# Differential attention: a running maximum over the chunks of keys, and two maps combined without dividing by the first sum

## The chip, the core and the metric

The kernel runs on one core of one Trainium2 chip. The metric is the device time of one execution in microseconds (us). Three runs of the kernel before gave 3016.61, 3018.57 and 3020.60 us, median 3018.57. The engines are named as the profile names them: PE (matmul) with PEld (its weight loads), DVE (vector), ACT (scalar, activations), POOL (general purpose, vector-like), and SP, whose queue issues all DMAs.

## What is computed

One decoder layer: a shared norm, one input projection, two token mixers side by side (sliding-window attention and differential attention), an output projection, cross-attention into a memory of 256 tokens, and a squared-ReLU MLP. Only the differential attention changes. It has 4 heads, 2048 tokens, two score maps per head and values of width 128:

```python
s = jnp.einsum('bqhcd,bkhcd->bhcqk', qblk, k) * scale      # c = 0, 1: two maps
s = jnp.where(mask, s, -jnp.inf)                           # causal
p = jax.nn.softmax(s, axis=-1)
a = p[:, :, 0] - lam * p[:, :, 1]
od = jnp.einsum('bhqk,bkhe->bqhe', a, v)
out_b = rms_norm(od, g_diff) * (1.0 - lam_init)            # per head, eps 1e-5
```

## The kernel before

The program runs in phases: the input projection, attention, the output projection (`phase_out`), cross-attention, the MLP up and down. Attention is cut into 32 units, one for a head `h` and a block `s` of 256 query tokens (`units`; heads 0 and 2 go through the blocks upwards, 1 and 3 downwards). A unit has one to four chunks `j` of at most 512 keys (`nch` chunks; two blocks of each head have one chunk, two have two, two three, two four) and two halves `t` of 128 queries.

**Scores** (`softmax`, L485 to L497). For every (j, t) and both maps c, PE makes scores into a PSUM bank `sc` (two matmuls, in the last chunk a third, L490, for the mask). DVE takes the row maximum, negated, into `nm` (L491), ACT makes exp(score - maximum) into `p[:, c]` and its row sum `l` (L492). There are four banks with the tag `s`; the score tiles of the window attention (`wsc`, L614) use them too. So the fifth score tile can only be begun when the exponential of the first has been read out of its bank.

**Weighing** (`weigh`). When all chunks of a unit are through, small DVE instructions on a few columns take the maximum over the chunks (L509), ACT makes the correction factors (L511), DVE the total sum and its reciprocal (L512 to L514), minus lambda into the second map's factor (L517), and the factors `scl` (L519). Then POOL multiplies the second map of every (j, t) by its factor (L524), and DVE adds the first map times its factor (L531). For the pairs in the table `POOL` both steps are done on POOL (L526, L527).

**Values** (`values`). PE transposes the combined map (L556), ACT and DVE copy it, in split form for some blocks (`af`; `ah` and `al`, L563, L142, L143), and PE multiplies by the values (L546). A sum of squares per token goes through POOL (L575) and PE (`pss`, L579) into `ss_d`. `phase_out` reads it back for every 512 tokens (`dss`), makes 1/sqrt(mean + eps) (`rsqrt_mean`, L157 to L163), stores it (`rs_d`), reads it back as rows (`rb`) and multiplies the attention output by it before the output projection (`po`, L807).

These steps, those of 32 window units (`window_softmax`, with the small L627 and L632, and `window_values`) and of 16 memory columns are laid out by due times in `phase_attention` (`at(...)`); a scheduler then sets the order in which the instructions stand on each engine. Each engine runs its own in that order.

Of the kernel before, what the change touches and what calls it, by code (L numbers as in the profile page):

```python
# [18 lines left out]
P = 128  # L19
# [47 lines left out]
class K:  # L67
# [77 lines left out]
            nc.scalar.activation(hi, src, AF.Copy, scale=scale)  # L145
            nc.vector.scalar_tensor_tensor(lo, src, scale, f(hi), op0=ALU.mult, op1=ALU.subtract)  # L146

    def rsqrt_mean(self, ss, n, out):

        nc = self.nc  # L150
        p, w = ss.shape
        if w == 512:
            v, y, t = (self.win(name=x) for x in ("rs_v", "rs_y", "rs_t"))
        else:
            v, y, t = (self.tiny_pool.tile([p, w], F32, name=x, tag=f"{x}{w}", bufs=1) for x in ("rs_v", "rs_y", "rs_t"))
        i = t.bitcast(I32)
        nc.vector.tensor_scalar(v, ss, 1.0 / n, EPS, op0=ALU.mult, op1=ALU.add)  # L157
        nc.vector.tensor_scalar(i, v.bitcast(I32), 1, None, op0=ALU.logical_shift_right)
        nc.vector.tensor_scalar(y.bitcast(I32), i, -1.0, float(0x5F3759DF), op0=ALU.mult, op1=ALU.add)
        for it in range(3):  # L160
# [277 lines left out]
def phase_attention(k, mt):  # L438
# [18 lines left out]
    def softmax(i, h, s, res):  # L457
# [17 lines left out]
        for j, w in enumerate(chunks):  # L475
            kt = kv[h, j][0]
            for t in range(2):
                last = j == nch - 1
                u = w - P if last and t == 0 else w
                um = max(u, 256)  # L480
                p = k.main([P, 2, 512], F32, name="p")
                for c in range(2):
                    sc = k.ps("s", name="sc")
                    for x in range(2):
                        mm = nc.tensor.matmul(  # L485
                            sc[:, :um], q[:, x, c, P * t : P * t + P], kt[:, c, :um], start=(x == 0), stop=(x == 1 and not last)
                        )
                        started.setdefault(i, mm)
                    if last:
                        nc.tensor.matmul(sc[:, u - P : u], k.identb, k.tri, start=False, stop=True)  # L490
                    nc.vector.tensor_reduce(nm[:, t, j, c : c + 1], sc[:, :u], axis=AX.X, op=ALU.max, negate=True)  # L491
                    nc.scalar.activation(  # L492
                        p[:, c, :u], sc[:, :u], AF.Exp, bias=nm[:, t, j, c : c + 1], accum_out=l[:, t, j, c : c + 1]
                    )
# [6 lines left out]
    def weigh(h, s, chunks, pt, nm, l):  # L501

        nch = len(chunks)
        sc = k.small([P, 2, 4, 2], "scl")[:, :, :nch]
        r = k.small([P, 2, 1, 2], "r")
        swap = "p t j c -> p t c j"
        if nch > 1:
            bm = k.small([P, 2, 1, 2], "bm")
            nc.vector.tensor_reduce(bm.rearrange(swap), nm.rearrange(swap), axis=AX.X, op=ALU.min)  # L509
            nc.vector.tensor_tensor(sc, bm.broadcast_to([P, 2, nch, 2]), nm, op=ALU.subtract)  # L510
            nc.scalar.activation(sc, sc, AF.Exp)  # L511
            nc.vector.tensor_tensor(l, l, sc, op=ALU.mult)  # L512
            nc.vector.tensor_reduce(r.rearrange(swap), l.rearrange(swap), axis=AX.X, op=ALU.add)
            nc.vector.reciprocal(r, r)  # L514
        else:
            nc.vector.reciprocal(r, l)
        nc.vector.tensor_scalar(r[:, :, :, 1], r[:, :, :, 1], k.nlam, None, op0=ALU.mult)  # L517
        if nch > 1:
            nc.vector.tensor_tensor(sc, sc, r.broadcast_to([P, 2, nch, 2]), op=ALU.mult)  # L519
        else:  # L520
            sc = r
        each = [(j, t, *pt[t, j]) for j in range(nch) for t in range(2)]
        for j, t, p, u in each:
            nc.gpsimd.tensor_tensor(p[:, 1, :u], p[:, 1, :u], sc[:, t, j, 1:2].broadcast_to([P, u]), op=ALU.mult)  # L524
            if (j, t) in POOL:
                nc.gpsimd.tensor_tensor(p[:, 0, :u], p[:, 0, :u], sc[:, t, j, 0:1].broadcast_to([P, u]), op=ALU.mult)  # L526
                nc.gpsimd.tensor_tensor(p[:, 0, :u], p[:, 0, :u], p[:, 1, :u], op=ALU.add)  # L527
        yield
        for j, t, p, u in each:
            if (j, t) not in POOL:  # L530
                nc.vector.scalar_tensor_tensor(  # L531
                    p[:, 0, :u], p[:, 0, :u], sc[:, t, j, 0:1], p[:, 1, :u], op0=ALU.mult, op1=ALU.add
                )
            yield
# [236 lines left out]
def phase_out(k, after):  # L771
# [6 lines left out]
    gd = k.small([P, 1], "gd", bufs=1)  # L778
    nc.vector.tensor_scalar(gd, k.g_diff, 1.0 - LAM_INIT, None, op0=ALU.mult)
    for c in CHUNKS:  # L780
        ss, rs = k.small([64, 32], "dss", bufs=2), k.small([64, 32], "drs", bufs=2)
        k.load(ss, k.ss_d[c].rearrange("h (a b) -> (h a) b", b=32))
        k.rsqrt_mean(ss, 128, rs)
        nc.sync.dma_start(k.rs_d[c].rearrange("o h (a b) -> (o h a) b", b=32), rs)
        o = [k.main([P, 2, 512], F32, name="o") for _ in range(4)]
        rb = [k.main([P, 2, 512], F32, name="rb") for _ in range(2)]
# [449 lines left out]
def build(nc, tc, a, out):  # L1236
# [3 lines left out]
    with ExitStack() as es:  # L1240
# [4 lines left out]
        k.vs_d = dram("vs_d", P, NT, P)  # L1245
        k.cs_d = dram("cs_d", 2, 32, S)
        k.ow_d, k.od_d = ([dram(f"{n}{i}", 4, P, 512) for i in range(4)] for n in ("ow_d", "od_d"))
        k.ss_d = [dram(f"ss_d{i}", 4, 512) for i in range(4)]
        k.rs_d = [dram(f"rs_d{i}", 1, 4, 512) for i in range(4)]
        k.kv_d = [[dram(f"kv_d{x}{i}", P, 4, MEM) for i in range(4)] for x in range(2)]  # L1250
        k.mt_d = [[dram(f"mt_d{x}{i}", P, 4, MEM) for i in range(2)] for x in range(2)]
# [100 lines left out]
```

## Time and profile before

| what | us |
|---|---|
| median of three runs | 3018.57 |
| the profiled execution | 3016.24 |
| its span, first to last instruction | 3014.5 |
| attention with its tail, 424 to 1036 us from the start | 612 |
| PE, DVE, ACT, POOL busy in these 612 us | 544.1, 491.1, 409.3, 378.2 |

A span row tells how long an engine was busy in a stretch; a wait row tells for whom an engine stood still; the chain of waits goes back from the last instruction to what released each step. The profiled execution lies 2.3 us below the median of the runs.

### The profile page before, as it was taken

The numbers are of one execution on the slowest core, as the hardware profiler recorded it, in microseconds if no ns is written. First come the engines' busy times: TensorE is split into PE (matmuls) and PEld (weight loads), VectorE is DVE, ScalarE is ACT, GpSimd is POOL, SyncE is SP. The second block draws the span as 40 slices with busy tenths as digits, with TensorE's granted clock in tenths as the row PEclk, the third lists the DMA queues.
The fourth block names the chain that finished last, engine by engine and source line by source line (L and its number), as shares of the span: only waits on it lengthen the run. The fifth ranks groups of instructions, "written<-read, shape, count | busy, mean of one in ns | idle before, by whom it ended". The sixth has DMA issues, their size and how long they took to land.

```text
span 3014.5 us, 38737 instructions
## 1 busy us (share of the span) xinstructions
PE 2882.1 (96%) x13740; PEld 2349.5 (78%) x13740; DVE 1762.1 (58%) x2918; ACT 1124.7 (37%) x2481; POOL 1161.8 (39%) x914
## 2 busy tenths in 40 slices
PE   8999988989999899999998999999999999999996
PEld 8978866666666688888886788778888888888886
DVE  5254448887788642422357765755556666666656
ACT  7221137666776521434324343533342111111113
POOL 0133336665666543112225666575551100110015
PEclk9999989999999999999998999999999999999997
DMA  8443264425342464211347553533345222212203
GB/s 313 133 179 127 108 195 123 126 72 154 114 122 85 156 203 166 93 49 44 117 134 247 181 178 112 177 124 112 110 151 214 73 68 77 77 60 74 77 7 112
DMA packets 223296, 380.21 MB, mean 126 GB/s; under 512 B 25312, under 2 KB 95104, under 8 KB 223104
## 3 DMA queue, kind: packets, MB, share of 16 engines
q1 hardware_dynamic: 223104, 377.75, 37.6%
q8 instruction: 108, 1.77, 0.2%
q14 instruction: 84, 0.69, 0.1%
HBM read 259.65 MB, written 116.98 MB: 125 GB/s over the span
## 4 chain that ended last, share of the span: by engine, by line
PE 61%; DVE 6%; DMA 3%; POOL 2%; issue 2%; ACT 1%; SPq 0%; POOLq 0%; DVEq 0%; ACTq 0%
PE pd L1194 23%; PE p L1102 18%; PE sc L871 6%; PE po L807 5%; PE po L995 4%; DMA xs<-x_d 1%; PE sc L485 1%; DVE p L531 1%; PE o L546 1%; PE wo L662 1%; PE pv L937 1%; PE pq L831 1%; DVE nm L491 1%; POOL p L524 1%; PE tt L556 1%
## 5 line engine op out<-in xcount | busy, mean ns | idle before, releaser
L1102 PE MATMUL p<-xh,w 128*128 128x512 f32 x1792 | 560.6, 394 | 22.4 <-DVE w L1093 11.2
L1198 DVE TENSOR_TENSOR acc<-pd,acc 128x512 f32<-128x512 f32 (+1 forms) x520 | 350.9, 681 | 254.0 <-PE pd L1194 251.4
L1102 PEld LDWEIGHTS p<-xh,w 128*128 128x128 f32 x1792 | 339.1, 190 | 99.3 <-DVE w L1093 13.7
L1194 PE MATMUL pd<-uh,wdh 128*128 128x512 f32 (+1 forms) x1040 | 401.7, 386 | 1.0 <-DVE acc L1198 1.0
L1194 PE MATMUL pd<-ul,wdh 128*128 128x512 f32 (+1 forms) x1040 | 401.2, 386 | 0.0
L1194 PE MATMUL pd<-uh,wdl 128*128 128x512 f32 (+1 forms) x1040 | 401.2, 386 | 0.0
L1102 PE MATMUL p<-xl,w 128*128 128x512 f32 x896 | 351.6, 392 | 0.0
L118 POOL TENSOR_TENSOR wdl<-wf,wdh 128x1024 fp32r<-128x1024 f32 x32 | 77.6, 2424 | 549.5 <-ACT wdh L117 543.6
L492 ACT ACTIVATE p<-sc,nm 128x512 f32<-128x512 f32 (+3 forms) x320 | 198.7, 627 | 94.1 <-DVE nm L491 92.8
L485 PE MATMUL sc<-kt,q 128*128 128x512 f32 (+2 forms) x640 | 198.6, 413 | 33.7 <-ACT p L492 23.1
L1194 PEld LDWEIGHTS pd<-uh,wdh 128*128 128x128 f32 x1040 | 195.4, 188 | 40.3 <-DVE acc L1198 1.2
L1194 PEld LDWEIGHTS pd<-ul,wdh 128*128 128x128 f32 x1040 | 195.4, 188 | 39.2
L1194 PEld LDWEIGHTS pd<-uh,wdl 128*128 128x128 f32 x1040 | 195.4, 188 | 39.2
L491 DVE TENSOR_REDUCE nm<-sc 128x1 f32<-128x512 f32 (+3 forms) x320 | 184.0, 600 | 53.4 <-PE sc L490 30.3
L1102 PEld LDWEIGHTS p<-xl,w 128*128 128x128 f32 x896 | 170.2, 190 | 35.8 <-issue 0.2
L485 PEld LDWEIGHTS sc<-kt,q 128*128 128x128 f32 x640 | 108.3, 198 | 85.5 <-ACT p L492 45.1
L524 POOL TENSOR_TENSOR p<-p,scl 128x512 f32<-128x512 f32 (+3 forms) x144 | 151.3, 1079 | 52.8 <-DVE scl L519 40.7
L142 ACT CAST uh<-uf 128x1024 fp32r<-128x1024 f32 x64 | 65.8, 1049 | 276.4 <-PE pd L1194 263.7
L306 PE MATMUL pa<-hh,wh 128*128 128x512 f32 x416 | 162.2, 390 | 0.2 <-DVE mt L146 0.2
L306 PE MATMUL pa<-hl,wh 128*128 128x512 f32 x416 | 162.1, 390 | 0.0
L306 PE MATMUL pa<-hh,wl 128*128 128x512 f32 x416 | 161.7, 389 | 0.0
L173 POOL TENSOR_TENSOR tot<-tot,sq 128x512 f32<-128x512 f32 x56 | 78.8, 1408 | 188.0 <-ACT sq L172 186.5
(266 smaller groups left out, 6046.0 us busy)
## 6 DMA issues: line engine op xcount, KB each, us to landing
wf<-w_up SPq DMA_DIRECT2D x64, 512.0 KB
u_d<-u SPq DMA_DIRECT2D x128, 256.0 KB
uf<-u_d SPq DMA_DIRECT2D x64, 512.0 KB
qk_d<-rot SPq DMA_DIRECT2D x96, 256.0 KB
x_d<-x SPq DMA_DIRECT2D x32, 512.0 KB
x<-x_d SPq DMA_DIRECT2D x32, 512.0 KB
xs<-x_d SPq DMA_DIRECT2D x32, 512.0 KB
wf<-w_down SPq DMA_DIRECT2D x32, 512.0 KB
```

Of the source, the lines that this page charges most:

```text
L173: getattr(nc, eng).tensor_tensor(total, total, sq, op=ALU.add)
L306: nc.tensor.matmul(pa, s_[d // 4][:, P * (d % 4) : P * (d % 4) + P], hs(m_, c, d), start=(d == 0 and i == 0), stop=(d == DT - 1 and i == 2),)
L485: mm = nc.tensor.matmul(sc[:, :um], q[:, x, c, P * t : P * t + P], kt[:, c, :um], start=(x == 0), stop=(x == 1 and not last))
L491: nc.vector.tensor_reduce(nm[:, t, j, c : c + 1], sc[:, :u], axis=AX.X, op=ALU.max, negate=True)
L492: nc.scalar.activation(p[:, c, :u], sc[:, :u], AF.Exp, bias=nm[:, t, j, c : c + 1], accum_out=l[:, t, j, c : c + 1])
L524: nc.gpsimd.tensor_tensor(p[:, 1, :u], p[:, 1, :u], sc[:, t, j, 1:2].broadcast_to([P, u]), op=ALU.mult)
L807: nc.tensor.matmul(po, wo[d][s_][:, P * n : P * n + P], m_[d // 2][:, d % 2], start=(d == 0 and z == 0), stop=(d == 7 and z == 2))
L871: nc.tensor.matmul(sc[n], x[s_][d][:, ts], wq[d][m_][:, 512 * n : 512 * n + 512], start=(d == 0 and z == 0), stop=(d == DT - 1 and z == 2))
L995: nc.tensor.matmul(po[i], vw[b][s_][:, P * n : P * n + P], m_[b], start=(b == 0 and z == 0), stop=(b == 7 and z == 2))
L1102: mm = nc.tensor.matmul(ps, t[:, s_, P * d : P * d + P], x[d][m_], start=(d == 0 and z == 0), stop=(d == 3 and z == 2))
L1194: nc.tensor.matmul(pd, w[ft][s_][:, P * n : P * n + P], u[m_][:, ft, ts], start=(ft == 0 and z == 0), stop=(ft == 1 and z == 2))
L1198: nc.vector.tensor_tensor(av, pd, av, op=ALU.add)
```

## The change

Maxima run on: from the second chunk on, DVE takes the smaller of this chunk's negated maxima and those of the chunk before (`nm`, both maps in one 128x2 instruction, 96 of them). So both maps' scores of a (j, t) are made first, then both maxima, then that minimum, then both exponentials. The last chunk's maximum is that of the whole row, so its correction factor is 1.

The maps are combined without dividing by the first sum: the result is l0 times the difference, with second factor -lambda * l0 / l1. The norm behind it takes up the factor if its eps is multiplied by l0 squared; l0 (`sums`) is stored to `l_d` by a DMA of 256 single numbers for each unit (32 of them), read back in `phase_out` (`dl`, 4 loads), squared and multiplied by eps. The last chunk is combined by one DVE instruction for each half; POOL's multiplications (L524) are 96 where they were 160. The table `POOL` names (2, 1) where it named (3, 1), and is asked only for chunks before the last, so 8 pairs of 256 columns go from POOL to one DVE instruction each (136 such instructions where there were 128).

```diff
-        nc.vector.tensor_scalar(v, ss, 1.0 / n, EPS, op0=ALU.mult, op1=ALU.add)
+        if eps is None:
+            nc.vector.tensor_scalar(v, ss, 1.0 / n, EPS, op0=ALU.mult, op1=ALU.add)
+        else:
+            nc.vector.scalar_tensor_tensor(v, ss, 1.0 / n, eps, op0=ALU.mult, op1=ALU.add)
...
+                both = []
                 for c in range(2):
                     sc = k.ps("s", name="sc")
+                    both.append(sc)
...
                     nc.vector.tensor_reduce(nm[:, t, j, c : c + 1], sc[:, :u], axis=AX.X, op=ALU.max, negate=True)
+                if j:
+                    nc.vector.tensor_tensor(nm[:, t, j], nm[:, t, j], nm[:, t, j - 1], op=ALU.min)
+                for c, sc in enumerate(both):
                     nc.scalar.activation(
...
-            nc.vector.tensor_reduce(bm.rearrange(swap), nm.rearrange(swap), axis=AX.X, op=ALU.min)
-            nc.vector.tensor_tensor(sc, bm.broadcast_to([P, 2, nch, 2]), nm, op=ALU.subtract)
+            nc.vector.tensor_tensor(sc, nm[:, :, nch - 1 :].broadcast_to([P, 2, nch - 1, 2]), nm[:, :, old], op=ALU.subtract)
...
-        nc.vector.tensor_scalar(r[:, :, :, 1], r[:, :, :, 1], k.nlam, None, op0=ALU.mult)
+        nc.vector.reciprocal(r[:, :, 1], sums[:, :, 1])
+        nc.vector.scalar_tensor_tensor(r[:, :, 1], r[:, :, 1], k.nlam, sums[:, :, 0], op0=ALU.mult, op1=ALU.mult)
...
+        nc.sync.dma_start(k.l_d[s // 2][h, cs].rearrange("(t p) -> p t", p=P), sums[:, :, 0])
         each = [(j, t, *pt[t, j]) for j in range(nch) for t in range(2)]
         for j, t, p, u in each:
-            nc.gpsimd.tensor_tensor(p[:, 1, :u], p[:, 1, :u], sc[:, t, j, 1:2].broadcast_to([P, u]), op=ALU.mult)
+            if j < nch - 1:
+                nc.gpsimd.tensor_tensor(p[:, 1, :u], p[:, 1, :u], sc[:, t, j, 1:2].broadcast_to([P, u]), op=ALU.mult)
...
         for j, t, p, u in each:
-            if (j, t) not in POOL:
+            if j == nch - 1:
+                nc.vector.scalar_tensor_tensor(p[:, 0, :u], p[:, 1, :u], r[:, t, 1:2], p[:, 0, :u], op0=ALU.mult, op1=ALU.add)
+            elif (j, t) not in POOL:
...
+        k.load(l, k.l_d[c].rearrange("h (a b) -> (h a) b", b=32))
+        nc.vector.scalar_tensor_tensor(l, l, EPS, l, op0=ALU.mult, op1=ALU.mult)
+        k.rsqrt_mean(ss, 128, rs, l)
```

What this does to the order shows at three places. Lines after the first edit are shifted in the changed kernel: L491 becomes L496, L492 becomes L500, L509 to L519 become L517 to L525, L531 becomes L538 (last chunk) and L540 (others), L118 and L143 stay.

On DVE at the end of the scores of head 0, block 6 (four chunks; `nm_4530`, in the changed kernel `nm_4532`, holds its maxima, `wl` belongs to a window unit), before:

```order
L491 TENSOR_REDUCE nm_4530<-sc_4736 128x1
L634 TENSOR_TENSOR wl_4636<-wl_4636,we_4637 128x4
L491 TENSOR_REDUCE nm_4530<-sc_4742 128x1
L635 RECIPROCAL wl_4636<-wl_4636 128x4
L491 TENSOR_REDUCE nm_4530<-sc_4750 128x1
L491 TENSOR_REDUCE nm_4530<-sc_4756 128x1
L509 TENSOR_REDUCE bm_4788<-nm_4530 128x4
```

and now:

```order
L498 TENSOR_TENSOR nm_4532<-nm_4532 128x2
L496 TENSOR_REDUCE nm_4532<-sc_4742 128x1
L496 TENSOR_REDUCE nm_4532<-sc_4747 128x1
L498 TENSOR_TENSOR nm_4532<-nm_4532 128x2
L496 TENSOR_REDUCE nm_4532<-sc_4757 128x1
L496 TENSOR_REDUCE nm_4532<-sc_4762 128x1
L498 TENSOR_TENSOR nm_4532<-nm_4532 128x2
L517 TENSOR_TENSOR scl_4795<-nm_4532 128x2x6
```

Two maxima are now followed by a minimum that reads both, and the reduction L509 is gone.

On ACT, in the first two chunks of the same unit (`sc` are score banks; `af` and `ah` are copies for the values of the unit before), before:

```order
L492 ACTIVATE p_4532,l_4531<-sc_4533,nm_4530 128x512
L563 COPY af_4488<-tt_4483 128x512
L492 ACTIVATE p_4532,l_4531<-sc_4538,nm_4530 128x512
L492 ACTIVATE p_4554,l_4531<-sc_4555,nm_4530 128x512
L142 CAST ah_4548<-tt_4543 128x512
L492 ACTIVATE p_4554,l_4531<-sc_4560,nm_4530 128x512
```

and now:

```order
L500 ACTIVATE p_4534,l_4533<-sc_4535,nm_4532 128x512
L500 ACTIVATE p_4534,l_4533<-sc_4539,nm_4532 128x512
L500 ACTIVATE p_4556,l_4533<-sc_4557,nm_4532 128x512
L500 ACTIVATE p_4556,l_4533<-sc_4561,nm_4532 128x512
L590 COPY row_4673<-pss_4671 1x256
L572 COPY af_4705<-tt_4700 128x512
L500 ACTIVATE p_4626,l_4533<-sc_4627,nm_4532 128x512
L500 ACTIVATE p_4626,l_4533<-sc_4631,nm_4532 128x512
```

Before, other work stood between the two exponentials of a pair; now they stand together.

On DVE at the end of attention, where the norm of the differential output begins (`dss` is the loaded sum of squares, `drs` the result, `al` the last split copy for the values, `wol` and `ol` belong to the output projection), before:

```order
L118 TENSOR_TENSOR wol<-wf,woh 128x1024
L163 SCALAR_TENSOR_TENSOR drs<-rs_t,rs_y 64x32
L157 TENSOR_SCALAR rs_v<-dss 64x32
L158 TENSOR_SCALAR rs_t<-rs_v 64x32
L159 TENSOR_SCALAR rs_y<-rs_t 64x32
L161 TENSOR_TENSOR rs_t<-rs_y 64x32
L162 SCALAR_TENSOR_TENSOR rs_t<-rs_t,rs_v 64x32
L163 SCALAR_TENSOR_TENSOR rs_y<-rs_t,rs_y 64x32
L161 TENSOR_TENSOR rs_t<-rs_y 64x32
L162 SCALAR_TENSOR_TENSOR rs_t<-rs_t,rs_v 64x32
L143 TENSOR_TENSOR al<-tt,ah 128x512
```

and now:

```order
L118 TENSOR_TENSOR wol<-wf,woh 128x1024
L166 SCALAR_TENSOR_TENSOR drs<-rs_t,rs_y 64x32
L143 TENSOR_TENSOR al<-tt,ah 128x512
L793 SCALAR_TENSOR_TENSOR dl<-dl 64x32
L143 TENSOR_TENSOR ol<-o,oh 128x1024
L160 SCALAR_TENSOR_TENSOR rs_v<-dss,dl 64x32
```

The last `al` stood behind the second `dss`; now it stands ahead of the second `dl`.

## Rows read from the trace of the kernel before

**Rows 1.** The page: the profiled execution's span.
```profile
span 3014.5 us, 38737 instructions
```

**Rows 2.** Busy time by stretch; columns are in the first line.
```profile
core 0: us, PE busy (x) PEld busy (x) DVE busy (x) ACT busy (x) POOL busy (x), PEclk, DMA share, GB/s
424.00:1036.00 612.00, 544.11 (x2974) 393.69 (x2973) 491.05 (x1025) 409.26 (x1260) 378.16 (x383) 0.95 0.41 120
...
719.00:1032.00 313.00, 282.20 (x1573) 204.03 (x1574) 252.18 (x531) 213.77 (x651) 195.25 (x201) 0.98 0.42 123
...
628.00:662.00 34.00, 27.15 (x134) 19.80 (x132) 30.53 (x52) 19.08 (x59) 25.59 (x27) 0.88 0.12 31
```

**Rows 3.** Waits, 424 to 1036 us: us in total, times, longest.
```profile
ACT p L492 <- DVE nm L491: 92.8, 90, 3.8
...
PEld sc L485 <- ACT p L492: 45.1, 51, 2.7
...
PE sc L485 <- ACT p L492: 23.1, 28, 2.5
...
DVE p L531 <- POOL p L524: 6.9, 10, 1.3
```

**Rows 4.** Groups by line, 424 to 1036: busy us, mean ns | idle before.
```profile
L491 DVE TENSOR_REDUCE nm<-sc 128x1 f32<-128x512 f32 x224 | 146.2, 679 | 27.9 <-PE sc L485 21.8 <-PE sc L490 5.7
L531 DVE SCALAR_TENSOR_TENSOR p<-p,scl 128x512 f32<-128x512 f32 x84 | 100.5, 1210 | 3.4 <-POOL p L524 3.3
...
L627 DVE TENSOR_TENSOR wnm<-wnm,nsink 128x2 f32<-128x2 f32 x64 | 21.7, 340 | 0.4
...
L524 POOL TENSOR_TENSOR p<-p,scl 128x512 f32<-128x512 f32 x108 | 123.0, 1163 | 52.8 <-DVE scl L519 40.7 <-DMA wk<-qk_d 7.4 <-DVE we L632 4.6
...
L526 POOL TENSOR_TENSOR p<-p,scl 128x256 f32<-128x256 f32 x8 | 7.1, 889 | 0.0
L527 POOL TENSOR_TENSOR p<-p 128x256 f32<-128x256 f32 x8 | 6.3, 784 | 0.0
```

**Rows 5.** Line 627, all instructions: duration ns min/median/max, first and last start.
```profile
L627 DVE TENSOR_TENSOR wnm<-wnm,nsink x64: 141/160/1839, 428.5 to 1000.7; 128x2 f32<-128x2 f32 x64
```

**Rows 6.** Timeline around 820 us: start, us, instruction [idle before].
```profile
815.55 3.72 DVE L531 SCALAR_TENSOR_TENSOR p<-p,scl 128x512 f32<-128x512 f32 x3
...
820.13 0.73 DVE L531 SCALAR_TENSOR_TENSOR p<-p,scl 128x512 f32<-128x512 f32 x1
820.79 1.27 DVE L491 TENSOR_REDUCE nm<-sc 128x1 f32<-128x512 f32 x2
...
821.50 0.69 ACT L492 ACTIVATE p<-sc,nm 128x512 f32<-128x512 f32 x1 [3.69 <-DVE nm L491]
...
822.33 0.73 PE L485 MATMUL sc<-kt,q 128*128 128x512 f32 x2 [0.78 <-ACT p L492]
```

**Rows 7.** The chain of waits, 719 to 1032 us, by line (shares of the stretch).
```profile
by line: PE sc L485 10.9%; DVE p L531 10.7%; PE o L546 8.5%; PE wo L662 6.9%; DVE nm L491 5.9%; issue 5.6%; POOL p L524 5.3%; PE tt L556 5.3%; ACT p L492 3.6%; PE pk L762 2.8%; DVE al L143 2.6%; DMA wq<-qk_d 2.2%; PE wsc L614 2.1%; DMA q<-q
```

**Rows 8.** Busy time by stretch of single lines: L531 (DVE), then L524 (POOL).
```profile
719.00:1032.00 313.00, 72.93 (x66) 0.98 0.42 123
...
424.00:1036.00 612.00, 163.37 (x160) 0.95 0.41 120
```

**Rows 9.** Timeline of the end of attention, by engine.
```profile
1025.05 0.38 PE L546 MATMUL o<-ah,v 128*128 128x256 f32 x1 [0.68 <-ACT ah L142]
1030.70 0.58 PE L546 MATMUL o<-al,v 128*128 128x256 f32 x1 [5.27 <-DVE al L143]
...
1087.55 1.05 PE L182 MATMUL col<-ones,tot 128*128 128x1 f32 x8 [0.60 <-POOL tot L173]
...
1028.37 0.17 DVE L157 TENSOR_SCALAR rs_v<-dss 64x32 f32<-64x32 f32 x1 [2.68 <-DMA dss<-ss_d]
...
1029.52 1.04 ACT L142 CAST oh<-o 128x1024 fp32r<-128x1024 f32 x1 [4.53 <-DMA o<-ow_d]
...
1025.13 0.27 SPq L582 DMA_DIRECT2D ss_d<-row  x1
```

More of the change, by code (lines that the diff above doesn't have):

```diff
@@ L42 @@
 CHUNKS = (3, 2, 1, 0)
-POOL = ((1, 1), (3, 1))
+POOL = ((1, 1), (2, 1))
 WHOLE = (0, 2, 4, 6)
@@ L146, in split, with rsqrt_mean @@
             nc.vector.scalar_tensor_tensor(lo, src, scale, f(hi), op0=ALU.mult, op1=ALU.subtract)
-    def rsqrt_mean(self, ss, n, out):
+    def rsqrt_mean(self, ss, n, out, eps=None):
         nc = self.nc
@@ L503, in weigh @@
         nch = len(chunks)
-        sc = k.small([P, 2, 4, 2], "scl")[:, :, :nch]
-        r = k.small([P, 2, 1, 2], "r")
-        swap = "p t j c -> p t c j"
+        r, sums = k.small([P, 2, 2], "r"), l[:, :, 0]
+        sc = None
         if nch > 1:
-            bm = k.small([P, 2, 1, 2], "bm")
-            nc.vector.tensor_reduce(bm.rearrange(swap), nm.rearrange(swap), axis=AX.X, op=ALU.min)
-            nc.vector.tensor_tensor(sc, bm.broadcast_to([P, 2, nch, 2]), nm, op=ALU.subtract)
+            old = slice(0, nch - 1)
+            sc = k.small([P, 2, 4, 2], "scl")[:, :, old]
+            nc.vector.tensor_tensor(sc, nm[:, :, nch - 1 :].broadcast_to([P, 2, nch - 1, 2]), nm[:, :, old], op=ALU.subtract)
@@ L511, in weigh @@
             nc.scalar.activation(sc, sc, AF.Exp)
[L512 to L516, printed above, removed]
-        nc.vector.tensor_scalar(r[:, :, :, 1], r[:, :, :, 1], k.nlam, None, op0=ALU.mult)
+            nc.vector.tensor_tensor(l[:, :, old], l[:, :, old], sc, op=ALU.mult)
+            sums = k.small([P, 2, 2], "ls")
@@ L518, in weigh @@
+            nc.vector.tensor_reduce(sums, l.rearrange("p t j c -> p t c j"), axis=AX.X, op=ALU.add)
+        nc.vector.reciprocal(r[:, :, 1], sums[:, :, 1])
+        nc.vector.scalar_tensor_tensor(r[:, :, 1], r[:, :, 1], k.nlam, sums[:, :, 0], op0=ALU.mult, op1=ALU.mult)
         if nch > 1:
-            nc.vector.tensor_tensor(sc, sc, r.broadcast_to([P, 2, nch, 2]), op=ALU.mult)
-        else:
-            sc = r
+            nc.vector.tensor_tensor(sc[:, :, :, 1], sc[:, :, :, 1], r[:, :, 1:].broadcast_to([P, 2, nch - 1]), op=ALU.mult)
@@ L522, in weigh @@
+        cs = slice(256 * (s % 2), 256 * (s % 2) + 256)
+        nc.sync.dma_start(k.l_d[s // 2][h, cs].rearrange("(t p) -> p t", p=P), sums[:, :, 0])
         each = [(j, t, *pt[t, j]) for j in range(nch) for t in range(2)]
         for j, t, p, u in each:
-            nc.gpsimd.tensor_tensor(p[:, 1, :u], p[:, 1, :u], sc[:, t, j, 1:2].broadcast_to([P, u]), op=ALU.mult)
-            if (j, t) in POOL:
-                nc.gpsimd.tensor_tensor(p[:, 0, :u], p[:, 0, :u], sc[:, t, j, 0:1].broadcast_to([P, u]), op=ALU.mult)
-                nc.gpsimd.tensor_tensor(p[:, 0, :u], p[:, 0, :u], p[:, 1, :u], op=ALU.add)
+            if j < nch - 1:
+                nc.gpsimd.tensor_tensor(p[:, 1, :u], p[:, 1, :u], sc[:, t, j, 1:2].broadcast_to([P, u]), op=ALU.mult)
+                if (j, t) in POOL:
+                    nc.gpsimd.tensor_tensor(p[:, 0, :u], p[:, 0, :u], sc[:, t, j, 0:1].broadcast_to([P, u]), op=ALU.mult)
+                    nc.gpsimd.tensor_tensor(p[:, 0, :u], p[:, 0, :u], p[:, 1, :u], op=ALU.add)
@@ L780, in phase_out @@
     for c in CHUNKS:
-        ss, rs = k.small([64, 32], "dss", bufs=2), k.small([64, 32], "drs", bufs=2)
+        ss, l, rs = (k.small([64, 32], n, bufs=b) for n, b in (("dss", 1), ("dl", 1), ("drs", 2)))
         k.load(ss, k.ss_d[c].rearrange("h (a b) -> (h a) b", b=32))
-        k.rsqrt_mean(ss, 128, rs)
+        k.load(l, k.l_d[c].rearrange("h (a b) -> (h a) b", b=32))
+        nc.vector.scalar_tensor_tensor(l, l, EPS, l, op0=ALU.mult, op1=ALU.mult)
+        k.rsqrt_mean(ss, 128, rs, l)
         nc.sync.dma_start(k.rs_d[c].rearrange("o h (a b) -> (o h a) b", b=32), rs)
@@ L1247, in build @@
         k.ow_d, k.od_d = ([dram(f"{n}{i}", 4, P, 512) for i in range(4)] for n in ("ow_d", "od_d"))
-        k.ss_d = [dram(f"ss_d{i}", 4, 512) for i in range(4)]
+        k.ss_d, k.l_d = ([dram(f"{n}{i}", 4, 512) for i in range(4)] for n in ("ss_d", "l_d"))
         k.rs_d = [dram(f"rs_d{i}", 1, 4, 512) for i in range(4)]
```

## The prediction

> **What bounds the kernel now.** The change lives in attention and its tail, 424 to 1036 us, so I read that stretch, not the page's shares. The profiled execution took 3016.24 us, 1.7 us more than its span [rows 1], and lies 2.3 us under the median of 3018.57; sums are made on it and shifted by 2.3 at the end. First the busy times by stretch [rows 2]: PE 544 of 612 us, DVE 491, ACT 409, POOL 378, the granted clock 0.95. No engine is full all the time. In the stretch of four-chunk units, 628 to 662, DVE is busy for 30.5 of 34 us while PE falls to 27.2 and its clock to 0.88. Then the waits [rows 3]: ACT stands still 92.8 us for row maxima, PE and its weight loads 23.1 and 45.1 us for exponentials, that is for a score bank; DVE waits only 6.9 us for POOL. So scores go round PE, DVE, ACT and back to PE through four banks, and the round is late because DVE is.
>
> One place shows it [rows 6]: three combinations hold DVE for 3.72 us, a fourth for 0.73, then come two maxima. ACT had waited 3.69 us for the first of them, and PE's next scores start 0.78 us late, right after its exponential. The chain of waits over the last 313 us of the stretch [rows 7] agrees: it runs through PE, but also through the combinations (10.7%), maxima (5.9%), POOL's multiplications (5.3%) and exponentials (3.6%). I price an edit by how much of its line's work lies on that chain, and scale from 313 to 612 us by 1.96.
>
> **The change part by part.**
>
> *Exponentials wait for both maps (cost).* In rows 6 the first exponential starts at 821.50, when the first of two maxima is done; now it also waits for the second, 0.59 us more (1.27 less one of 0.68, the 679 ns of rows 4), and for the new minimum. The trace has no such minimum, but the same operation on the same shape in L627: 141 ns at least, 160 median, 340 mean [rows 4, 5], the difference being POOL's doing (below). With the dependent start that is 0.2 to 0.4 us, so a bank comes free 0.25 us later (only the minimum counts, because ACT was late anyhow) to 1.0 us later (both count). I take 0.7, nearer the upper end since rows 6 is the commoner picture. Queued behind the waiting exponential on ACT are the copies for the values, which used to stand between the two of a pair; behind the late bank waits PE. On the chain lie 3.6% of 313 us, 11.3 us, of exponentials of 0.69 us [rows 6, 7]: 16, times 1.96 is 32. **+22 us** (8 to 32).
>
> *The other minima (cost).* 96 are added, 32 counted; 64 at 0.3 us are 19 us of DVE, less 24 small reductions (L509) taken out at L627's 0.16, 4 us: 15. The rest of the small work in the weighing is exchanged like for like, priced at 0. DVE's lines in rows 7 make 19.2% of 313 us, 60 of its 252 busy [rows 2], so 0.24 of DVE's work lies on the chain: **+4** (0 to 8).
>
> *Eight more combinations on DVE (cost).* 136 for 128, at 1.21 us [rows 4]: 9.7 us. Of L531's 72.9 us in the 313 [rows 8], 10.7%, 33.5 us, lie on the chain, 0.46: **+4.5** (3 at the lone 0.73 us, 10 if all count).
>
> *POOL's work taken out (gain).* L524 is busy for 163.4 us with 160 [rows 8]; 96 of 512 columns stay, at 1163 ns [rows 4] 111.6; so 52 us go. Its 5.3% of 313 us, 16.6, are 0.20 of its share of that stretch (163.4 x 313/612 = 83.6). **-10**, down to -13 if the pairs L526 and L527 (13.4 us, rows 4) count as much, -3 if only the one- and two-chunk units gain, since what goes stands last in each burst.
>
> *DVE freed from POOL (gain).* A combination of 512 columns takes 0.73 us alone and 1.21 on average [rows 4, 6]: 84 x 0.48 = 40 us of hindrance. POOL's 378 us shrink by 52 + 13, 17%, so 7 us of it go, 0.46 of them on the chain: **-3** (0 to -9). What the rows show is that two-operand DVE work stretches beside POOL's (a 128x2 one from 0.14 to 1.84 us [rows 5]), while a maximum, read from PSUM, keeps its 0.68. The Trainium skill, in SBUF — State Buffer, section SBUF: two separate sides, calls the pair of ports that DVE and GpSimd share an exclusive lock: who comes second is blocked for the whole instruction. By that rule the hindrance goes with the meetings, and units whose POOL burst disappears lose all of it, which would be nearer -9 than -3; the sum keeps -3.
>
> *The tail (gain).* Before, the last split copy `al` stood behind a `dss` instruction that waited 2.68 us for its load, and PE stood still for 5.27 us [rows 9]. Now `al` stands ahead. Next in line is `oh`, which ACT begins at 1029.52 when its load has landed [rows 9], so PE's output projection can come perhaps 1 us sooner for it and a few more for what is done meanwhile; two sums `pss` now stand ahead of it. **-3** (-5 to +2).
>
> *DMAs (nothing).* 32 stores from SP at 0.27 us of issue (a small store, rows 9) wait for `sums`; behind them in SP's queue stand loads of later units' q, started three units ahead, and that lead hides them. The four loads `dl` and two DVE instructions for each lie in a chain behind which PE has work until its first gap at 1087.55 [rows 9]. Without that cover they would cost a load's wait, 2.7 us, for each of four; I put 0 to +3.
>
> Sum: 22 + 4 + 4.5 - 10 - 3 - 3 = +14.5, say **+14**, giving 3030 on the profiled execution and **3032 us** on the median. All lower ends together give -19, all upper ones +52; neither is likely at once.
>
> **The rivals.**
>
> *Faster: POOL and its hold on DVE set the pace of the weighing.* Place: the bursts of L524 and the combinations among them, 16% of the chain [rows 7]. For it: 40 us of hindrance, and whole bursts vanish in one-chunk units. Price: the bank delay hidden by transposes and values that the new order puts between scores (a third of 22, +7), other minima +2, combinations +4.5, POOL -13, freed DVE -9, tail -5: -13.5, so 3005. This is the case that the rule of the port lock speaks for. Against it: DVE's waits for POOL are 6.9 us [rows 3]. It decides if ACT's wait for maxima does not grow.
>
> *No change:* each exponential only 0.25 us later (+8) and the rest as summed, 8 + 4 + 4.5 - 10 - 3 - 3 = +0.5: 3019. For it: ACT is often behind by itself.
>
> *Much slower:* the banks' delay meets every four-chunk stretch, where DVE already has 30.5 of 34 us [rows 2], and PE's gaps pull its clock to the 0.88 seen there. Price: 32 + 8 + 10 - 3 - 3 = +44, less where ACT catches up, some +40: 3059.
>
> **How the numbers follow.** Forecast near 3032: 0.40. Much slower: 0.13. Faster: 0.29. No change: 0.18. Faster or slower is meant by over 0.2%, 6 us, about what a measurement of this kernel can tell. So slower 0.53, same 0.18, faster 0.29. The range of 8 in 10 leaves out the far part of the two outer cases: 2998 to 3060; the forecast's own is 3025 to 3048.
>
> **What would show it.** In the trace after: the 96 minima at about 0.3 us; ACT's wait for the maximum or the minimum up from 92.8 us towards 110; PE's and its loads' waits for exponentials above 68 us together; L524 near 112 us; combinations of 512 columns below 1.21 us but well above 0.73; the gap of 5.27 us gone; from 1036 us on everything as before. Wrong would be a bank wait that stays at 68 us or falls, combinations near 0.8 us, or a stage longer for another reason, such as loads of q that come late behind the new stores.

## The result and the profile of the changed kernel

The changed kernel takes 3133.85 us (median of 4 runs), the kernel before 3019.59 beside it: a ratio of 1.0384, with a 95% interval of 1.0368 to 1.0400. That is 114 us slower; 14 were forecast, and the time lies outside the range of 2998 to 3060.

The page's span and the main DMA queue's share (37.6% before) come first, then the busy time of two stretches (columns as in [rows 2]). The first goes from the first scores to just past the first matmuls `po` of the output projection, which start at 1152.60 us; the second goes from there to the end.

```profile
span 3136.5 us, 38835 instructions
...
q1 hardware_dynamic: 232128, 377.82, 39.2%
```
```profile
424.00:1156.00 732.00, 585.38 (x2978) 419.42 (x2978) 496.09 (x1106) 410.74 (x1263) 319.64 (x305) 0.89 0.47 100
```
```profile
1152.00:3136.00 1984.00, 1930.89 (x8680) 1599.92 (x8680) 1088.66 (x1592) 582.89 (x975) 676.77 (x440) 0.98 0.35 118
```

Everything that was lost was lost ahead of `po`: the stretch of 612 us [rows 2] takes 732, and what follows takes as long as before (1980.5 us from 1156 on; before, 1978.5 from 1036 on). DVE and ACT have hardly more to do than they had (491 and 409 us), POOL less (378). PE does the same matmuls, but is busy 41 us longer (585 for 544) while the granted clock falls from 0.95 to 0.89 (544 times 0.95/0.89 is 581, an estimate), and it is not busy for 147 us in place of 68. These two, 41 and 79, are the 120.

The waits of that stretch, 424 to 1156 us (us in total, times, longest; L490 are the scores, L496 the maxima, L498 the new minima, L500 the exponentials; before in [rows 3]):

```profile
PE sc L490 <- DMA q<-qk_d: 42.8, 14, 7.3
PE sc L490 <- ACT p L500: 27.7, 30, 3.8
PE sc L490 <- DMA kt<-qk_d: 11.8, 2, 6.7
PE sc L490 <- DMA wf<-w_ckv: 9.9, 1, 9.9
...
PEld sc L490 <- ACT p L500: 49.5, 59, 4.2
...
ACT p L500 <- DVE nm L496: 93.7, 42, 13.1
...
ACT p L500 <- DVE nm L498: 30.6, 30, 3.3
```

Two things are new. PE stands still for loads, 42.8 us for q and 64.5 with `kt` and `wf` (3.5 and 0.8 for q and `kt` before). And ACT waits 124.3 us for a maximum or a minimum, 92.8 before; some of these waits, the one of 13.1 us for one, hold a stop of PE for a load. The instructions themselves are nearly as foreseen (groups by line, columns as in [rows 4]): the minima at 253 ns, POOL's 96 multiplications at 1255 for 1163, the combinations of 512 columns ahead of the last chunk (L540) at 1130 ns for 1210.

```profile
L531 POOL TENSOR_TENSOR p<-p,scl 128x512 f32<-128x512 f32 x96 | 117.8, 1255 | 32.2 <-DVE scl L525 31.7
...
L540 DVE SCALAR_TENSOR_TENSOR p<-p,scl 128x512 f32<-128x512 f32 x72 | 80.8, 1130 | 0.0
...
L498 DVE TENSOR_TENSOR nm<-nm 128x2 f32<-128x2 f32 x96 | 24.2, 253 | 1.3
```

One store shows where the loads went. The busy times around it, by 2 us:

```profile
core 0: us, PE busy (x) PEld busy (x) DVE busy (x) ACT busy (x) POOL busy (x), PEclk, DMA share, GB/s
...
802.00:804.00 2.00, 2.00 (x13) 1.86 (x13) 1.08 (x4) 1.45 (x5) 0.54 (x1) 0.81 0.41 67
804.00:806.00 2.00, 1.04 (x6) 0.43 (x4) 1.93 (x5) 0.57 (x2) 1.50 (x2) 1.00 0.66 143
806.00:808.00 2.00, 0.29 (x2) 0.00 (x0) 0.43 (x1) 0.36 (x1) 0.00 (x0) 1.00 0.54 32
808.00:810.00 2.00, 0.00 (x0) 0.00 (x0) 0.00 (x0) 0.00 (x0) 0.00 (x0) 0.90 0.78 31
810.00:812.00 2.00, 0.00 (x0) 0.00 (x0) 0.00 (x0) 0.00 (x0) 0.00 (x0) 0.50 0.54 67
```

and the timeline, SP's rows first, then what follows the stop:

```profile
802.52 0.38 SPq L527 DMA_DIRECT2D l_d<-l  x1
802.94 0.58 SPq L104 DMA_DIRECT2D q<-qk_d  x1
```
```profile
813.60 2.08 PE L490 MATMUL sc<-kt,q 128*128 128x512 f32 x4 [7.31 <-DMA q<-qk_d]
814.43 1.89 DVE L496 TENSOR_REDUCE nm<-sc 128x1 f32<-128x512 f32 x3 [8.00 <-PE sc L490]
...
815.16 0.69 ACT L500 ACTIVATE p<-sc,nm 128x512 f32<-128x512 f32 x1 [8.43 <-DVE nm L496]
```

SP issues the store of 256 single numbers in 0.38 us and the next load of q right behind it. Some 3 us later the DMAs are still more than half busy and move 31 GB/s. From 808 to 812 no engine works at all, PE has stood still for 7.31 us when q lands, and the clock has dropped to 0.50, the lower of its two levels. The trace's records of single DMA packets tell more. The store's own 256 packets take 0.01 us each and are through by 804. Behind them packets of 2048 bytes take up to 4.1 us each. From 424 to 1040 us, packets of at most 4 KB that take over 1.5 us number 293 here and none in the kernel before.

### The profile page after: what moved, and what is told of

It is laid out like the page before. It is cut to its first block, busy times and chain, and to the rows that moved or that the text cites. A ratio compares the mean times of both kernels' runs of the same rounds, so it can differ in the third digit from the quotient of the medians.

```text
span 3136.5 us, 38835 instructions
## 1 busy us (share of the span) xinstructions
PE 2922.9 (93%) x13740; PEld 2375.6 (76%) x13740; DVE 1764.1 (56%) x3002; ACT 1126.3 (36%) x2481; POOL 1101.4 (35%) x834
## 4 chain that ended last, share of the span: by engine, by line
PE 58%; DVE 2%; DMA 2%; POOL 1%; issue 1%; ACT 1%; SPq 0%; POOLq 0%; DVEq 0%; ACTq 0%
PE pd L1205 22%; PE p L1113 18%; PE sc L882 6%; PE po L818 5%; PE po L1006 5%; PE pv L948 1%; DMA xs<-x_d 1%; PE pq L842 1%; PE pt L910 0%; PE col L185 0%; DVE xl L146 0%; POOL o L1193 0%; DVE rs_t L164 0%; DMA ss_d<-row 0%; DMA rb<-rs_d 0%
## 5 line engine op out<-in xcount | busy, mean ns | idle before, releaser
L490 PE MATMUL sc<-kt,q 128*128 128x512 f32 (+2 forms) x640 | 212.8, 438 | 107.1 <-DMA q<-qk_d 42.8
L118 POOL TENSOR_TENSOR wdl<-wf,wdh 128x1024 fp32r<-128x1024 f32 x32 | 77.5, 2423 | 549.5 <-ACT wdh L117 543.7
L496 DVE TENSOR_REDUCE nm<-sc 128x1 f32<-128x512 f32 (+3 forms) x320 | 186.2, 604 | 141.9 <-PE sc L495 79.4
L500 ACT ACTIVATE p<-sc,nm 128x512 f32<-128x512 f32 (+3 forms) x320 | 197.1, 623 | 127.3 <-DVE nm L496 93.7
L490 PEld LDWEIGHTS sc<-kt,q 128*128 128x128 f32 x640 | 116.6, 213 | 158.0 <-ACT p L500 49.5
L1127 ACT ACTIVATE u<-u 128x512 f32<-128x512 f32 x128 | 80.9, 632 | 183.9 <-DVE u L1126 183.8
L882 PE MATMUL sc<-wq,xh 128*128 128x512 f32 x512 | 144.8, 394 | 0.0
```

The source lines that it names most:

```text
L118: getattr(nc, eng).tensor_tensor(lo, wf, f(hi), op=ALU.subtract)
L490: mm = nc.tensor.matmul(sc[:, :um], q[:, x, c, P * t : P * t + P], kt[:, c, :um], start=(x == 0), stop=(x == 1 and not last))
L500: nc.scalar.activation(p[:, c, :u], sc[:, :u], AF.Exp, bias=nm[:, t, j, c : c + 1], accum_out=l[:, t, j, c : c + 1])
L882: nc.tensor.matmul(sc[n], x[s_][d][:, ts], wq[d][m_][:, 512 * n : 512 * n + 512], start=(d == 0 and z == 0), stop=(d == DT - 1 and z == 2))
L1127: nc.scalar.activation(u, u, AF.Square)
```

## The experiments

The theories at first: **S**, the stores clog the DMAs (S1 because 128 writes of 4 bytes fall side by side into the same stretches of 512 bytes, S2 by their number); **Q**, SP stands waiting for the sums, and the loads behind it start late; **B**, exponentials that wait for both maps hold the score banks. Differences below are to the kernel before, measured beside each run (3014 to 3019 us); the changed kernel has +114.

**What the stores cost.** Four runs, of which r1, r3 and r4 leave out epsilon times the square of the first sum.

r1, no store and no load:
```diff
-        nc.sync.dma_start(k.l_d[s // 2][h, cs].rearrange("(t p) -> p t", p=P), sums[:, :, 0])
```


> The changed kernel without the 32 stores of the first sums to memory and without their loads; the norm keeps its constant eps, so the factor of the first sum is left out of it. Theory S (the stores of 256 single numbers clog the DMA engines, and q and keys come late): near the kernel before, 3015 to 3040 us, PE's wait for q under 10 us where it is 63 us. Theory B (both maps' exponentials wait for two maxima and a minimum, score banks come free late): still 3110 us or more. Theory Q (SP stands waiting for the sums, and loads behind the store are issued late): as S.

r2, the kernel before with a store of the same shape that nobody reads:
```diff
+        nc.sync.dma_start(k.l_d[s // 2][h, cs].rearrange("(t p) -> p t", p=P), r[:, :, 0, 0])
```


> The kernel before with nothing added but 32 stores of 256 single numbers (the first map's reciprocal sums), which nobody reads. Theory S: some 80 to 120 us slower than before, 3100 to 3140 us. Theory B: 3015 to 3025 us, since maxima and exponentials are as before. Theory Q: slower as well, by part of it.

r3, the store cut to two numbers, so that SP waits as before:
```diff
+        nc.sync.dma_start(k.l_d[s // 2][h : h + 1, cs.start : cs.start + 2], sums[0:1, :, 0])
```


> The changed kernel with each of the 32 stores cut to two numbers of one partition; SP waits for the same sums at the same place, the loads are taken out and the norm keeps its constant eps, so the factor of the first sum is left out of it. Theory S: as the run without stores, within 10 us. Theory Q: as the changed kernel, 3110 us or more. Theory B: as the changed kernel.

r4, all 256 numbers, each into a row of 512 bytes of its own:
```diff
+        nc.sync.dma_start(k.l_s[8 * h + s].rearrange("t p e -> p t e")[:, :, 0:1], sums[:, :, 0:1])
```


> The changed kernel with the 32 stores of 256 single numbers going to addresses 512 bytes apart instead of next to each other; not read back, the norm keeps its constant eps, so the factor of the first sum is left out of it. If the writes hinder each other because they fall into the same 512 bytes (theory S1): near the run without stores, within 20 us. If it is their number that clogs the engines (theory S2): as the changed kernel, 3100 us or more.

Measured: r1 3068.06 (+50; ratio 1.0168, 1.0153 to 1.0183), r2 3088.53 (+71; 1.0241, 1.0220 to 1.0261), r3 3068.66 (+51; 1.0167, 1.0150 to 1.0184), r4 3071.31 (+54; 1.0178, 1.0162 to 1.0195). So the stores, with their loads, cost 64 us in the changed kernel, and stores alone 71 in the kernel before, where nothing else was edited (the scheduler moved some of the order). r1 fell between what S and B had expected, so both have a part; r2 was slower as S says, by less than the 80 us at least that were expected. It is not SP's waiting (r3 has it and is as r1). Nor is it the number of writes or their size: r4 has as many of 4 bytes, and costs 3 us more than r1. The order of the instructions is not the reason either: in the traces r3 and r4 differ from the changed kernel in 22 rows on PE, of some 13,700 in each. S1 stands, with one limit: r4's writes go to 32 tensors in place of 4, so distance and place changed together. The main queue's rows of r2 and r4 (packets, MB, share of the engines' time) have the same count of packets:

```profile
q1 hardware_dynamic: 231808, 377.79, 39.6%
```
```profile
q1 hardware_dynamic: 231808, 377.79, 37.5%
```

Of the slow packets counted above, r2 has 267, r4 3 and r1 none. What the loads `dl` cost by themselves was not tried. Around a store of r4 (issued at 743.53 us) the same columns read:

```profile
743.00:745.00 2.00, 2.00 (x15) 1.77 (x13) 1.11 (x4) 1.96 (x7) 0.79 (x1) 1.00 0.84 223
745.00:747.00 2.00, 2.00 (x19) 1.97 (x18) 1.39 (x4) 1.08 (x4) 0.43 (x1) 1.00 0.71 145
747.00:749.00 2.00, 2.00 (x10) 1.00 (x9) 0.00 (x0) 0.43 (x1) 1.52 (x4) 1.00 1.06 316
```

PE never stops, and the DMAs move 145 to 316 GB/s where the changed kernel's fall to 31. In r2, PE's wait for q is what grew most, from 3.5 us in the kernel before:

```profile
PE sc L485 <- DMA q<-qk_d: 34.3, 13, 6.2
```

The Trainium skill, DMA: Bandwidth & Descriptors, section Specifications, puts transfers of at least 512 bytes as the condition for full rate and says that smaller ones are read, modified and written. By size alone r4 would pay as the changed kernel does; the runs say that what costs is small writes side by side.

**The whole computation with another way for the sums.** r5 collects them in SBUF and stores rows of 512 bytes; r7 has besides a minimum for each map.
```diff
+        pl = k.ps("o", [16, P], name="pl")
+        nc.tensor.transpose(pl, k.l_all[:, c, :, 0], k.ident)
+        nc.scalar.copy(lr, pl)
+        nc.sync.dma_start(k.l_d[c].rearrange("h (a b) -> (h a) b", b=P), lr)
```


> The whole computation of the changed kernel, epsilon included; only the way of the first sums to DRAM is changed: they are collected in SBUF, and for each 512 tokens one TensorE transpose, one ScalarE copy and one store of 16 rows of 512 bytes take the place of 8 stores of 256 single numbers. Theory S1 (single numbers that fall into the same 512 bytes clog the DMAs): near the run without any store, 3068 us (3062 to 3076). If it is not the form of the store that costs but that the sums leave at all: 3100 or more.


```diff
+                    if j:
+                        nc.vector.tensor_tensor(nm[:, t, j, c : c + 1], nm[:, t, j, c : c + 1], nm[:, t, j - 1, c : c + 1], op=ALU.min)
                     nc.scalar.activation(
```


> The whole computation of the changed kernel, sums stored in rows; the minimum is taken for each map by itself (192 of 128x1 in place of 96 of 128x2), so that a map's exponential follows its own maximum again. If the order of the pair is the cost of ~50 us: 3018 to 3035. If the minimum in the chain is: twice as many, 3068 or more. If the new weighing is: 3060 to 3070.

Measured: 3128.38 (+111; 1.0367, 1.0350 to 1.0384) and 3112.23 (+95; 1.0318, 1.0301 to 1.0334): a miss, by a new fault. In r5 the scores' stretch ends at 1077.7, like r1's at 1084.7. But transposition, store and load now stand at each chunk of the output projection, and PE waits there (1060 to 1300 us, r5):

```profile
POOL o L811 <- DMA rb<-rs_d: 65.2, 7, 21.4
...
PE po L822 <- ACT oh L145: 62.6, 4, 18.7
```

So r10 does without DRAM: TensorE adds the term to the row of sums of squares.
```diff
+            nc.tensor.matmul(pss[:, P * t : P * t + P], kv[h, s, "le"][:, t : t + 1], k.identb, start=False, stop=(t == 1))
```


> The whole computation of the changed kernel with nothing stored: epsilon times the square of the first sum is added by TensorE to the row of sums of squares (two matmuls of 1x128 in bfloat16 for each unit), so the stores, the four loads and the separate step in the output projection are gone. The run with rows had the scores' stage of 652 us (the run without a store 661) but an output projection 67 us longer, whose first matmuls waited for the sums' way through DRAM. Theory (stores of single numbers 65 us, running maxima the rest): 3062 to 3072, stage about 661, projection 594 to 598. If the sums cost on any way: 3100 or more.

r12 is r10 with a minimum for each map.

> As the run with epsilon on TensorE, but with a minimum for each map (192 of 128x1), so that an exponential waits for its own map alone. Theory B (an exponential waits for the other map's score and maximum, and this holds the banks): the stage near the 632 us that the run with rows and a minimum per map showed, so 3036 to 3045. If the number of minima on VectorE is what costs: above 3068.

Measured: r10 3079.30 (+61; 1.0207, 1.0185 to 1.0229), a little above its range, and r12 3045.49 (+28; 1.0103, 1.0075 to 1.0131). With nothing stored the change is 53 us cheaper, and letting an exponential wait for its own map alone saves another 34.

**The running maxima.** r6 takes them alone, with the weighing of before; r8 was to show the order of the pair.
```diff
+                if j:
+                    nc.vector.tensor_tensor(nm[:, t, j], nm[:, t, j], nm[:, t, j - 1], op=ALU.min)
+                for c, sc in enumerate(both):
```


> The kernel before with the running maxima alone: both scores of a chunk, both maxima, the minimum with the chunk before, then both exponentials; the weighing stays as before (divided by both sums, eight multiplications on GpSimd), with the last chunk's maximum as the common one; no store. Theory B (the exponentials that wait for both maps hold the score banks, and that is the ~50 us left without the store): 3060 to 3075. If the ~50 us come from the new weighing (last chunk unscaled, combinations moved to VectorE): 3018 to 3025, as the kernel before. If they come from both: between, 3035 to 3050.


```diff
+                for c, sc in enumerate(both):
```


> The kernel before with the order of the pair alone: both scores, both maxima, then both exponentials, each with its own chunk's maximum (no minimum, weighing as before). If the order of the pair is the cost (the first map's bank is held for the second map's score and maximum): like the run with the running maxima, 3055 to 3070. If the added minimum of 128x2 between the maximum and the exponentials is the cost: 3018 to 3030.

r6: 3109.71 (+92.5; 1.0303, 1.0283 to 1.0322), more than expected. r8: 3015.74 (0.9998, 0.9986 to 1.0010), and it tells nothing about pairs: its order on PE, DVE and ACT is row for row that of the kernel before, because the first exponential still depends on its own maximum alone and the scheduler lays it out the same way. It shows only how well a time repeats. The pair is bound together by the minimum of 128x2, not by the order of the lines. One place in r6:

```profile
640.30 4.26 POOL L527 TENSOR_TENSOR p<-p,scl 128x512 f32<-128x512 f32 x4
...
640.80 1.28 DVE L493 TENSOR_REDUCE nm<-sc 128x1 f32<-128x512 f32 x2
...
642.00 0.79 DVE L495 TENSOR_TENSOR nm<-nm 128x2 f32<-128x2 f32 x1
...
642.83 0.69 ACT L497 ACTIVATE p<-sc,nm 128x512 f32<-128x512 f32 x1 [3.76 <-DVE nm L495]
```

Both maxima are done at 642.08. The minimum, at best 0.12 us in this run, takes 0.79 beside POOL's burst, and the exponential starts at 642.83. Its own maximum was done some 0.6 us before the second.

r13 puts the minima at the same places of the program, read by the weighing only. r16 is r6 with a minimum for each map.
```diff
+                    nc.vector.tensor_tensor(bm[:, t, 0], nm[:, t, j], bm[:, t, 0] if j > 1 else nm[:, t, 0], op=ALU.min)
```


> The kernel before with the same 96 minima of 128x2 at the same places on VectorE's queue, but beside the path: the exponentials keep their own chunk's maximum, and the running minimum is read only by the weighing, in place of its one reduction over the chunks. Theory B (the wait of the exponential costs, not the instruction): 3016 to 3026. If the 96 instructions on VectorE cost by themselves (96 of 0.25 us, 24 us): 3040 or more.

> The kernel before with running maxima alone, a minimum for each map (192 of 128x1), the weighing as before with the last chunk's maximum as the common one. If the wait for the other map is what made 3110 of the run with a minimum for both maps: 3030 to 3055. If the weighing of before makes running maxima dearer by ~40 us whichever way they wait: 3075 to 3090.

r13: 3023.16 (+5; 1.0018, 1.0007 to 1.0028). r16: 3060.81 (+41; 1.0138, 1.0122 to 1.0154), 6 us above the one theory's range and 14 below the other's: waiting for the other map too, with the order made for it, makes 51 of r6's 92.5 us, and a minimum per map is not cheap either.

**The new weighing.** r15 has it without any minimum ahead of an exponential. Each chunk keeps its own maximum, and the last chunk is left unscaled all the same, so r15 leaves out a step that the result needs; its instructions in the weighing are those of the changed kernel, with the reduction over the chunks and epsilon on TensorE besides.
```diff
+            nc.vector.tensor_reduce(bm.rearrange(swap), nm.rearrange(swap), axis=AX.X, op=ALU.min)
+            nc.vector.tensor_tensor(sc, bm.broadcast_to([P, 2, nch - 1, 2]), nm[:, :, old], op=ALU.subtract)
```


> The new weighing with no minimum ahead of any exponential: every chunk keeps its own maximum, and one reduction over the chunks in the weighing gives the common one, as before; epsilon on TensorE. The last chunk of a unit is left unscaled though its exponentials stand on their own maximum, so the scaling of the last chunk is left out of the computation. If the ~27 us left are the waits for the minimum: 3010 to 3024. If they are the new weighing (or the two matmuls): 3038 to 3050.

r14 has only the missing division, r11 the new weighing with minima in the last chunk alone, r18 the new weighing with the last chunk's first map scaled by ScalarE.
```diff
+        nc.vector.scalar_tensor_tensor(r[:, :, :, 1], r[:, :, :, 1], k.nlam, sums[:, :, :, 0], op0=ALU.mult, op1=ALU.mult)
```


> The kernel before with one part of the change: the maps are combined without dividing by the first sum (epsilon times its square is added by TensorE); own maxima for every chunk, all eight multiplications on GpSimd, GpSimd's combinations at the same chunks as before. If neither the missing division nor the two matmuls cost or give: 3016 to 3024. If the two matmuls of 1x128 for each unit cost (the run with epsilon on TensorE was 11 us above the run without a store): 3027 to 3035.


```diff
+                    if last and j:
+                        nc.vector.tensor_reduce(nm[:, t, j, c : c + 1], nm[:, t, : j + 1, c], axis=AX.X, op=ALU.min)
```


> The new weighing of the changed kernel (last chunk unscaled, not divided by the first sum, epsilon on TensorE, whole computation), but chunks before the last keep their own maxima, and only in the last chunk of a unit a minimum over the chunks, per map, stands between the maximum and the exponential (96 in all). Theory B says that each exponential that waits longer costs: 2 of 3 waits fewer than with a minimum per map in all chunks, so the stage at 608 to 625 us and 3015 to 3035. If the weighing itself costs and not the wait: no better than with a minimum per map everywhere, about 3040. If the smaller weighing (144 multiplications on GpSimd become 96) is worth something by itself: below 3015.


```diff
+            if j == nch - 1:
+                nc.scalar.activation(p[:, 0, :u], p[:, 0, :u], AF.Copy, scale=sc[:, t, j, 0:1])
```


> The new weighing without running maxima, the whole computation: own maxima in every chunk, the common one by one reduction in the weighing, not divided by the first sum (epsilon on TensorE); the last chunk's first map is scaled by ScalarE (48 multiplications more there), its second map by VectorE's combination, so that GpSimd has the 96 multiplications of the changed kernel. The run with the last chunk left unscaled took 3003, the one with all multiplications on GpSimd 3014. If what counts is GpSimd's work: 3003 to 3010. If ScalarE's 48 multiplications (at about 0.6 us, 28 us) come onto the path: 3015 to 3035.

r15: 3002.69 (-17; 0.9946, 0.9929 to 0.9962). r14: 3013.64 (0.9992, 0.9978 to 1.0007), no difference. r11: 3046.01 (+28; 1.0092, 1.0071 to 1.0113), which by what was expected of it would speak against the weighing; r15 rules that out. r18: 3033.02 (+19; 1.0055, 1.0042 to 1.0069). So the gain of the weighing lies in the last chunk, which GpSimd no longer multiplies (with 8 pairs that moved to DVE), not in the division: r14 has only the missing division, and gains nothing. It vanishes if ScalarE, on whose copies and exponentials PE waits, takes the multiplications over, and no complete kernel among these beats the kernel before by more than can be measured.

Put together, differences to the kernel before (r15 leaves out the last chunk's scaling):

| | no minimum ahead of the exponential | one for each map | one for both maps |
|---|---|---|---|
| weighing of before | 0 | +41 (r16) | +92.5 (r6) |
| new weighing, epsilon on TensorE | -17 (r15) | +28 (r12) | +61 (r10) |

The waits of PE's weight loads and matmuls for an exponential rise along the second line: r15, r12, r10, each in its own stretch (before: [rows 3], 68.2 together).

```profile
PEld sc L485 <- ACT p L492: 35.7, 50, 1.8
...
PE sc L485 <- ACT p L492: 14.9, 25, 1.4
```
```profile
PEld sc L485 <- ACT p L494: 46.7, 54, 4.2
...
PE sc L485 <- ACT p L494: 26.0, 30, 3.3
```
```profile
PEld sc L487 <- ACT p L497: 58.5, 62, 5.2
...
PE sc L487 <- ACT p L497: 37.7, 34, 4.8
```

Together 50.6, 72.7 and 96.2 us: the bank comes free later with each step. So does the exponential start later. From the end of a maximum to the start of its exponential it is 129, 305 and 426 us, summed over all 320 (worked out from the traces' starts and ends); the kernel before has 139, the changed kernel 428.

**The wait or the order.** Each of these dependences also makes the scheduler lay out another order. r17 is r13 with a dependence of the exponentials on the minimum that the scheduler sees and the chip does not wait for.
```diff
+                    if j:
+                        k.behind(ex, mn)
```


> The run with the minima beside the path (3023 us), and the scheduler is told besides that both exponentials come behind the minimum, as in the run with running maxima (3110 us); on the chip they wait for their own maximum alone, since the dependence carries no semaphore. The order of the instructions then differs from that of the kernel before about as much as with running maxima. If the wait itself costs: 3016 to 3035. If the order that the scheduler makes of it costs: 3080 to 3115.

Measured: 3044.20 (+30; 1.0094, 1.0074 to 1.0115), between the two theories. In its trace the exponentials wait 102.3 us for maxima and never for a minimum. Of r6's 92.5 us, 5 go with the minima's own time (r13), 25 more with an order made for the wait, and about 62 are left for the wait itself. This split is an estimate from one order, and r17's is not that of r6: the two traces differ in 1,244 rows on PE, where r6 differs from the kernel before in 1,850 (both kernels' rows counted, of some 13,700 each). How much of r6's cost is its own order stays open. An order that differs need not be dear: r14's differs from that of the kernel before in 1,300 rows on PE, r17's in 1,648, and r14 costs nothing.

## Why the prediction was wrong, point by point

The three parts of the 114 us: -17 for the new weighing (r15), +78 for the minima ahead of both exponentials (r10 less r15: the wait, the minima's own time and the order made for them), +53 for the stores (the changed kernel less r10). The direction and the stretch were right, the sum was not. (The prediction's "All lower ends together" is wrong too: they add up to -16, not -19.) Most of its signs came, the waits of PE and its loads for exponentials above 68 us (27.7 and 49.5) among them.

**DMAs, "nothing" (0 to +3): 53 to 64.** This step had the mechanism wrong, and made about half of the miss. It priced a store by SP's issue, and that price nearly held, 0.37 us for 0.27 (24 of the 32 stores):

```profile
L527 SPq DMA_DIRECT2D l_d<-ls x24: 360/372/551, 462.9 to 1108.4; - x24
```

But the cost of a store is not at its issue. The text said that the lead of three units hides the loads behind; q's loads came late all the same, because the DMAs were slow with the packets that came behind a store, for some 8 us. It did name "loads of q that come late behind the new stores" as what would prove it wrong, yet gave this no chance and no price among the rivals. The step should have asked what the store looks like to a DMA engine: 256 writes of 4 bytes, side by side.

**Exponentials that wait for both maps, +22 (8 to 32): 78, the minima's own time among them.** This term made the other half. The mechanism was right, its size was not, in both factors. The delay was put at 0.7 us. By the sums over 320 exponentials, 139 us before and 428 now, it is 1.5 us more for each of the 192 that now wait, if all of it is theirs. The count was put at 32 exponentials, from the share that they have of the old chain of waits (3.6%); at 1.5 us these would have made 48. A share of the old chain says what an edit gives back if a line gets shorter; a line that gets longer can pull the chain onto itself. Some of the 78 may be the scheduler's answer to the new dependence (r17), which the sum had no term for: on PE r10 differs from r15 in 1,748 rows.

**The other minima, +4: +5 (r13).** About right, in price and in duration (253 ns for 0.3 us). These 5 are part of the 78 above.

**Combinations +4.5, POOL -10, freed DVE -3, tail -3, together -11.5: -17 (r15).** Right in sign, a third too small. POOL's 96 multiplications take 117.8 us for 111.6 expected, the combinations ahead of the last chunk 1.13 us, as foreseen below 1.21 and far above 0.73. r14, with all of GpSimd's multiplications, gains nothing, so the gain goes with those of the last chunk. The tail's gap of 5.27 us [rows 9] is gone; gaps of 2.39 and 2.44 us stand there now (timeline of PE, changed kernel):

```profile
1146.52 0.58 PE L555 MATMUL o<-al,v 128*128 128x256 f32 x1 [2.39 <-DVE al L143]
...
1152.60 0.80 PE L818 MATMUL po<-oh,woh 128*128 128x512 f32 x1 [2.44 <-ACT oh L142]
```

**The rivals.** "Much slower" had the right mechanism for the banks, with 32 us for what cost 78, and no stores. "Faster" was right that the weighing gives something, and wrong that other work hides the banks' delay.

**Open.** Why minima in the last chunk alone (r11: 96 reductions of 0.15 us) cost as much as 192 in all chunks (r12) is not settled. The delay does not tell: the sum over all 320 exponentials is 179 us in r11, 305 in r12, 129 in r15. The orders differ as well, so an order may cost more here than r17's 25 us say.

## What to carry to other kernels

Ask of a store how many writes it makes and where they fall; its issue time says nothing about what it does to the loads that come behind. Do not price an added dependence in a round trip between engines by the share that the waiting line has on the old chain: 22 us were put so, and 78 came. Its delay times its count is no price either, since 289 us of added delay (428 less 139) came with these 78; a run with the dependence and one without it gave the price. And compare the order of an experiment's instructions with that of the kernel that it varies. A reordering that leaves the order the same tests nothing (r8); r3 and r4 could tell what a store costs because nearly everything else kept its place; an order that is very different tests more than was meant (r17).

## What the runs showed of the hardware

- A store of 256 separate 4-byte numbers side by side slows the loads behind it for some 8 us: 31 GB/s with the DMAs 0.54 to 0.78 busy, packets of 2048 bytes at up to 4.1 us while its own take 0.01 us each; 64 to 71 us for 32 such stores. Spread to one number in 512 bytes, as many writes cost 3 us. Distances in between were not tried, nor what happens at the memory.
- A minimum of 128x2 on DVE takes 0.14 to 0.16 us alone (71 of 96 in the changed kernel) and up to 2.10 where it meets GpSimd's instructions (the other 25):

```profile
L498 DVE TENSOR_TENSOR nm<-nm x96: 140/160/2096, 458.5 to 1106.1; 128x2 f32<-128x2 f32 x96
```

- Waits of PE cost more than their length: of the 120 us that the stretch grew, 41 are the same matmuls at a lower mean clock.
